# Two of three token tiles of the inner activation transposed by DMA instead of by TensorE

## The chip, the cores and the metric

The kernel runs on one core of one Trainium2 chip. Time is device time in microseconds (us). The kernel before took 1952.08 us, the median of three runs (1951.8 to 1953.06). The profile shown is of one further execution of the same program.

## The reference

One layer of a hybrid backbone is computed in float32 for 128 context tokens and 256 latent tokens, so 384 tokens with a model width of 2048: adaLN modulation, a mixing sub-layer (gated linear attention beside a Fourier branch), and a SwiGLU feed-forward sub-layer of hidden width 5632. Only the last of these bears on the change:

```python
h = rmsnorm(x, lw['norm_pre_ffn']) * (1.0 + sc2) + sh2
ff = (jax.nn.silu(h @ lw['w_ffn_gate']) * (h @ lw['w_ffn_up'])) @ lw['w_ffn_down']
x = x + ga2 * rmsnorm(ff, lw['norm_post_ffn'])
```

## The kernel before

Every float32 matrix product is made of three TensorE products: each operand is parted into a rounded high part and the rest (`whi`, `wlo` for weights), and high by high, high by low and low by high are added up. ScalarE rounds the high part (line 1430), VectorE subtracts to get the low part (line 1441), so each weight tile of 128x1024 costs one ScalarE pass and one VectorE pass before TensorE may use it.

The hidden width of the feed-forward part is worked through in eleven chunks of 512 columns, `c` = 0 to 10. From `c` = 1 on, the gate and up products of a chunk and the down products of the chunk before it are interleaved in one list, `steps` (lines 1338 to 1357). A step takes one weight tile. Its kind says what it computes. Kinds `A`, `B`, `C`, `E`, `F`, `G`, `H`, four steps each, are the gate and up products, arranged with sums and differences of token tiles and weights in the manner of Strassen's method, so that fewer products are needed. Kinds `D`, `DA` to `DH` are down products of chunk `c - 1`. The order in the part that matters is: H0, D6, H1, H2, D7, H3 of one chunk and then A0, A1, A2, A3, B0, B1, D4 of the next. A step of A has 12 matmuls (two token tiles), a step of H has 6, a step of D has 18.

The gate and up products come out with tokens on partitions and hidden columns along the free dimension. Once silu and the product are done, three tiles of 128 tokens x 512 float32 stand in the work tiles `g0`, `g1` and `s5` (token tiles 0, 1 and 2). The down product needs them the other way round, with hidden columns on partitions. `turn_hid` (lines 1591 to 1599) does that: four TensorE transposes of 128x128 float32 into one PSUM bank (line 1596, tile `ptr`), and then ScalarE and VectorE part the result into `hid_hi` and `hid_lo` (line 1598). In the main loop that is called behind the matmuls of A1, A2 and A3 for token tiles 1, 2 and 0 (line 1782). `hid_sums` (lines 1601 to 1610) forms sums and differences of the turned tiles 1 and 2 for the down product, and `hid_sums_lo` their low part.

The order on TensorE, ScalarE, VectorE and GpSimd is written out by hand; SyncE's is planned by the framework. Each step begins with `grab2` (line 1452): it takes the step's weight tile from a list of ready ones, issues what loads have room (`load_more`, on SyncE's queue), and calls `split_next` (line 1420), which makes the whi and wlo of a weight tile that is used three steps later. There are four buffers of each, so the ScalarE pass waits until TensorE has finished with the buffer of the step before. Work that is not weights is put off in a list, `pend`, and `split_next` takes three or four items from its head in each step (`settle_pend`), between the ScalarE pass and the VectorE pass. So an item that holds ScalarE or VectorE delays the weight passes behind it on that engine, in order.

Weights for A and B come through ten resident slots (loads `u`, line 1407), the others through two buffers `raw` (line 1399). `sum1` (line 1413) subtracts one resident slot from another on VectorE before the steps of B. The down sums of most chunks are added up in device memory by accumulating transfers that GpSimd issues (line 1642) out of tiles that ScalarE copies from PSUM (line 1638). VectorE also does the last adaLN map between all this (line 1474).

Of the kernel before, what the change touches and what calls it, by code (L numbers as in the profile page):

```python
# [11 lines left out]
F32 = mybir.dt.float32  # L12
F32R = mybir.dt.float32r
U32 = mybir.dt.uint32
AF = mybir.ActivationFunctionType
ALU = mybir.AluOpType
PSUM = bass.MemoryType.PSUM
# [3 lines left out]
P = 128  # L21
# [4 lines left out]
T = TC + TL  # L26
# [8 lines left out]
FC = 4  # L35
# [61 lines left out]
def tile_step(ctx: ExitStack, tc: tile.TileContext, a, o):  # L97
    nc = tc.nc
    PE, ACT, DVE, POOL, SP = nc.tensor, nc.scalar, nc.vector, nc.gpsimd, nc.sync
# [215 lines left out]
    psm = ctx.enter_context(tc.tile_pool(name="psm", bufs=3, space=PSUM))  # L315
    pss = ctx.enter_context(tc.tile_pool(name="pss", bufs=5, space=PSUM))
    with ExitStack() as s:
# [114 lines left out]
        for k in range(KT):  # L432
            sq = qs[k] if k < 2 else scr[:, 4 + k % 4, :]
# [178 lines left out]
    with ExitStack() as s:  # L612
# [9 lines left out]
        for c in range(2):  # L622
            src = a["a2"][:, 512 * c : 512 * c + 512]
# [192 lines left out]
        for c in range(2):  # L816

            dst = a2.rearrange("p (h d j) -> p d h j", d=2, j=P)[:, c]
# [29 lines left out]
    with ExitStack() as s:  # L848
# [166 lines left out]
        for b, i in mix_order:  # L1015
# [29 lines left out]
    with ExitStack() as s:  # L1045
# [49 lines left out]
        for i in range(KT):  # L1095
            p = psm.tile([P, T], F32, tag="mm", name="pmm")
# [193 lines left out]
        dt = {}  # L1290
# [11 lines left out]
        hid = hid_of()  # L1302
# [9 lines left out]
        pend, now = [], []  # L1312
# [26 lines left out]
        LAST = NFC - 1  # L1339
# [251 lines left out]
        def turn_hid(dst, t, pool, tag):  # L1591

            pt = pool.tile([P, FC, P], F32, tag=tag, name="ptr")
            src = (g0, g1, s5)[t]
            for j in range(FC):
                PE.transpose(pt[:, j, :], src[:, j * P : (j + 1) * P], ident)  # L1596
            hi, lo = (x[:, :, t * P : (t + 1) * P] for x in dst)
            pend.extend([lambda: ACT.copy(hi, pt), lambda: DVE.tensor_sub(lo, pt, hi.bitcast(F32))])  # L1598
# [88 lines left out]
        for kind, c, i in steps:  # L1687
            last_c = c == NFC - 1 and kind == "D"
            if last_c and hid_last is not None and x1b is None:
                while pend:  # L1690
                    pend.pop(0)()
                x1b = actp.tile([P, KT, T], F32, tag="A_hi", name="x1b")
                for q in range(4):
                    SP.dma_start(x1b[:, 4 * q : 4 * q + 4, :], x1_d[:, 4 * q : 4 * q + 4, :])
                ACT.activation(tmp1, eps_t, AF.Sqrt)
            if last_c and done >= 2:
                late_w.append(grab2())
                if len(late_w) == 4:
                    while pend:
                        pend.pop(0)()  # L1700
                continue
            if kind == "D":
                w = grab2()
                n, kh = i // 2, i % 2
                if kh == 0:
                    while pend:
                        pend.pop(0)()

                    pool, tag = (pss, "side") if done % 2 or (c, n) == (NFC - 2, 3) else (psm, "mm")
                    ts = (0, 1, 2) if last_c else (1, 2, 0)  # L1710
                    pd_tiles = {t: pool.tile([P, 512], F32, tag=tag, name="pdn") for t in ts}
                    d_live[0] += 3
                h = hid_last if last_c else hid
                todo = [
                    (pd_tiles[t], [[x[:, 2 * kh + m, t * P : (t + 1) * P] for m in range(2)] for x in h], mov_d, kh == 0, kh == 1)
                    for t in ts
                ]
                products(w, todo)
                if kh == 1:
                    if not last_c:  # L1720
                        for t in range(3):
                            if c < LAST - 1:
                                pend.append(lambda k=10 + 3 * (n - 2) + t, p=pd_tiles[t], c=c: to_sums(k, p, c))
                            else:
                                pend.append(lambda u=unit(t, n), p=pd_tiles[t]: out(u, p))
                    else:
                        for t in range(3):
                            pend.append(lambda t=t, n=n, p=pd_tiles[t], d=done: add_last(t, n, p, d))
                        if done == 1:
                            pend.append(lambda: DVE.tensor_add(r3, ssq[:, :, 0], ssq[:, :, 1]))  # L1730
                        done += 1
                if (c, i) == (NFC - 2, 6):

                    while pend:
                        pend.pop(0)()
                    hid_last = tuple(actp.tile([P, FC, T], F32R, tag=t, name="hidE") for t in ("C_hi", "C_lo"))
                    for t in range(3):
                        turn_hid(hid_last, t, psm, "mm")
                    for x in (0, 2, 4, 1, 3, 5):
                        pend[x]()  # L1740
                    pend.clear()
            elif kind[0] == "D":
                w = grab2()
                while pend:
                    pend.pop(0)()
                todo = []
                for n, stat, first, last in of_d[kind]():
                    if first:
                        d_bank[n] = psm.tile([P, 512], F32, tag="mm", name="pds")
                        d_live[0] += 1  # L1750
                    todo.append((d_bank[n], stat, mov_d, first, last))
                    if last:
                        pend.append(lambda k=PROD.index(n), p=d_bank[n], c=c: to_sums(k, p, c))
                products(w, todo, by_tile=kind in ("DB", "DC"))
            else:
                w = grab2()
                if kind == "H" and i == 0:
                    while pend:
# [12 lines left out]
                if (kind, c, i) == ("B", LAST, 0):  # L1771
                    while pend:
                        pend.pop(0)()
                    back = sums_back()
                if kind == "A" and i:
                    if c == 1 and i == 2:
                        while pend:
                            pend.pop(0)()
                        d_tiles()
                        load_more()  # L1780
                    if c > 1:
                        hid_pt.append(turn_hid(hid, i % 3, psm, "mm"))
                    if c < LAST and i == 2:
                        if c == 1:
                            f = dt["full"]
                            pend.append(lambda: DVE.tensor_add(f, hid[0][:, :, P:T].bitcast(F32), hid[1][:, :, P:T].bitcast(F32)))
                            pend.extend(hid_sums(f[:, :, 0:P], f[:, :, P:], DVE.tensor_copy))
                        else:
                            pend.extend(hid_sums(*hid_pt))
                    if i == 3:  # L1790
                        if c < LAST:
                            pend.insert(len(pend) - 1 if c > 1 else len(pend), hid_sums_lo)
                        hid_pt.clear()
                if (kind == "A" and i < 2) if turned[0] else c < LAST and kind + str(i) in ada_at:
# [177 lines left out]
```

## Time and profile before

| What | Value |
|---|---|
| median of 3 runs | 1952.08 us (1951.8 to 1953.06) |
| the profiled execution | 1951.26 us, span 1949.5 us |
| TensorE matmul busy | 1932.7 us, 99% of the span |
| VectorE busy | 1641.2 us, 84% |
| ScalarE busy | 1015.1 us, 52% |
| GpSimd busy | 145.2 us, 7% |
| TensorE transposes of `turn_hid` | 120, first at 1065.5 us, last at 1897.3 us |
| granted TensorE clock | 0.999 |

The profile is of one execution. PE is TensorE's matmuls, PEld its weight loads, DVE is VectorE, ACT is ScalarE, POOL is GpSimd, SPq the queue of SyncE. "whi<-u" names the tile written and the tile read. In lists of instructions in order of time, the first column is the start and the second the duration, both in us; an "x4" at the end of a row says that four like instructions were merged; a bracket gives idle time of the engine just before, and who ended it. The chain of work that ended last follows the end of the program back, at each step to what released it, and so says what the time was spent on.

### The profile page before, as it was taken

Reading aid. Unit: us, or ns where it says so; the run is one execution under the profiler, and the core shown is the slowest. Engines: PE = TensorE matmul, PEld = TensorE weight load, DVE = VectorE, ACT = ScalarE, POOL = GpSimd, SP = SyncE. Lnnn points to the kernel's source line nnn. Section 1 sums busy time; section 2 is a strip of 40 time slices with the busy share of each in tenths; the row PEclk is TensorE's granted clock in tenths of the full one; section 3 lists DMA queues with packets and bytes.
Section 4 is the critical chain, followed back from the end, with each engine's and each line's share of the span. In section 5 each row is a group of like instructions: output and inputs, shape, how many; then the busy total and the mean of one; then the engine's idle time right before and its main releaser. Section 6 shows DMA issues by size and latency. Waiting matters only on the chain.

```text
span 1949.5 us, 28077 instructions
## 1 busy us (share of the span) xinstructions
PE 1932.7 (99%) x10506; PEld 1712.5 (88%) x10506; DVE 1641.2 (84%) x2059; ACT 1015.1 (52%) x1477; POOL 145.2 (7%) x171
## 2 busy tenths in 40 slices
PE   8999999999999999999999999999999999999998
PEld 5779999999999999999988888888888888888886
DVE  5569888879876797978799999999999999988876
ACT  4233454554336655447455655555565565656445
POOL 0000000000000000004000111111111120211001
PEclk9999999999999999999999999999999999999999
DMA  9978677767754687655538686877868695959564
GB/s 390 370 262 265 228 251 230 229 224 257 252 189 159 213 277 247 211 175 182 169 128 261 148 252 153 236 185 204 213 193 225 175 236 168 248 128 241 151 205 130
DMA packets 217640, 422.05 MB, mean 216 GB/s; under 512 B 16796, under 2 KB 121436, under 8 KB 213152
## 3 DMA queue, kind: packets, MB, share of 16 engines
q1 hardware_dynamic: 199072, 386.70, 59.3%
q0 software_dynamic: 18432, 33.56, 11.4%
q8 instruction: 82, 1.34, 0.3%
q14 instruction: 54, 0.44, 0.1%
HBM read 365.68 MB, written 54.53 MB: 216 GB/s over the span
## 4 chain that ended last, share of the span: by engine, by line
PE 95%; DVE 2%; DMA 1%; ACT 1%; issue 0%; SPq 0%; POOL 0%; DVEq 0%; ACTq 0%; POOLq 0%
PE pmm L258 35%; PE pgu L1532 30%; PE pdn L1532 10%; PE pds L1532 7%; PE pv L398 3%; PE pgm L381 1%; PE pf L996 1%; DMA slab<-in_w_ada 1%; PE px L416 1%; PE pmm L1251 1%; PE ptr L1596 1%; PE pf L997 1%; PE bk L1532 1%; PE po L645 1%; DVE wlo L1441 0%
## 5 line engine op out<-in xcount | busy, mean ns | idle before, releaser
L258 PE MATMUL pmm<-A_hi,whi 128*128 128x384 f32 x1200 | 404.3, 337 | 0.0
L258 PE MATMUL pmm<-A_hi,wlo 128*128 128x384 f32 x1200 | 401.4, 334 | 0.0
L258 PE MATMUL pmm<-A_lo,whi 128*128 128x384 f32 x1200 | 401.3, 334 | 0.0
L1430 ACT CAST whi<-u 128x1024 fp32r<-128x1024 f32 x200 | 209.5, 1053 | 156.3 <-PE pgu L1532 53.7
L224 ACT CAST whi<-raw 128x1024 fp32r<-128x1024 f32 x181 | 189.7, 1051 | 176.1 <-DMA raw<-in_w_gate 53.3
L225 DVE TENSOR_TENSOR wlo<-raw,whi 128x1024 fp32r<-128x1024 f32 x179 | 217.9, 1220 | 52.3 <-ACT whi L224 51.9
L1430 ACT CAST whi<-raw 128x1024 fp32r<-128x1024 f32 x157 | 165.5, 1054 | 181.4 <-DMA raw<-in_w_d 48.5
L1441 DVE TENSOR_TENSOR wlo<-u,whi 128x1024 fp32r<-128x1024 f32 x200 | 242.2, 1218 | 17.4 <-ACT whi L1430 16.8
L1532 PE MATMUL pgu<-whi,A_hi 128*128 128x512 f32 x640 | 252.0, 394 | 0.0
L1532 PE MATMUL pgu<-whi,A_lo 128*128 128x512 f32 x640 | 249.5, 390 | 0.0
L258 PEld LDWEIGHTS pmm<-A_hi,whi 128*128 128x128 f32 x1200 | 225.3, 188 | 2.9 <-issue 1.4
L572 DVE SCALAR_TENSOR_TENSOR adacc<-adaw,spad,adacc 128x1024 f32<-128x1024 f32 x180 | 222.7, 1278 | 3.4 <-DMA adaw<-in_w_ada 3.2
L258 PEld LDWEIGHTS pmm<-A_lo,whi 128*128 128x128 f32 x1200 | 225.4, 188 | 0.2
L258 PEld LDWEIGHTS pmm<-A_hi,wlo 128*128 128x128 f32 x1200 | 225.2, 188 | 0.0
L1441 DVE TENSOR_TENSOR wlo<-raw,whi 128x1024 fp32r<-128x1024 f32 x157 | 191.3, 1219 | 17.6 <-ACT whi L1430 17.4
L1532 PE MATMUL pgu<-wlo,A_hi 128*128 128x512 f32 x640 | 185.9, 389 | 0.0
L1532 PEld LDWEIGHTS pgu<-whi,A_hi 128*128 128x128 f32 x640 | 120.1, 188 | 26.7 <-issue 1.2
L1532 PEld LDWEIGHTS pgu<-wlo,A_hi 128*128 128x128 f32 x640 | 120.2, 188 | 25.5
L1532 PEld LDWEIGHTS pgu<-whi,A_lo 128*128 128x128 f32 x640 | 120.2, 188 | 24.2
L1532 PE MATMUL pgu<-whi,S 128*128 128x512 f32 x400 | 117.6, 391 | 0.0
L1642 POOL DMA_DIRECT2D sums_d<-dw x64 | 58.6, 950 | 644.0 <-ACT dw L1638 638.7
L1532 PE MATMUL pdn<-whi,hid_hi 128*128 128x512 f32 x264 | 102.9, 390 | 0.2 <-DVE hid_lo L1598 0.2
(402 smaller groups left out, 3268.0 us busy)
## 6 DMA issues: line engine op xcount, KB each, us to landing
adaw<-in_w_ada SPq DMA_DIRECT2D x96, 512.0 KB, 4.2
raw<-in_w_d SPq DMA_DIRECT2D x70, 512.0 KB, 3.8
slab<-in_w_ada SPq DMA_DIRECT2D x32, 1024.0 KB
raw<-in_w_gate SPq DMA_DIRECT2D x64, 512.0 KB, 4.6
raw<-in_w_g SPq DMA_DIRECT2D x48, 512.0 KB, 4.2
raw<-in_w_u SPq DMA_DIRECT2D x48, 512.0 KB, 6.9
raw<-in_w_in SPq DMA_DIRECT2D x44, 512.0 KB, 5.0
u<-in_w_u SPq DMA_DIRECT2D x40, 512.0 KB, 7.5
```

Source lines behind the costliest of these rows:

```text
L224: ACT.copy(hi, raw)
L225: sub = lambda: eng.tensor_sub(lo, raw, hi.bitcast(F32))
L258: PE.matmul(dst, w[wi][:, k * n + n0 : k * n + n0 + P], x[xi][:, k0 + k, :], start=first and k == 0 and j == 0, stop=last and k == kts - 1 ...
L381: PE.matmul(pgv[q : q + 32, :], spad[:, k, :], slab[k // (KT // 2)][:, k % (KT // 2), :], start=k < 4, stop=k >= KT - 4,)
L398: PE.matmul(pv[2 * t + g], hT[x_][:, kb, t * P : (t + 1) * P], w_[:, g * 512 : (g + 1) * 512], start=kb == 0 and j == 0, stop=kb == KT - 1 ...
L416: PE.matmul(px, w_[:, u * P : (u + 1) * P], hT[x_][:, kb, :], start=j == 0, stop=j == 2)
L572: DVE.scalar_tensor_tensor(acc[:, c, :], w, spad[:, k, c : c + 1], acc[:, c, :], op0=ALU.mult, op1=ALU.add,)
L645: PE.matmul(dst, w[wi], x[xi], start=first and j == 0, stop=last and j == 2)
L1430: ACT.copy(hi, src)
L1441: DVE.tensor_sub(lo, src, hi.bitcast(F32))
L1532: PE.matmul(dst, stat[x_][m], mov(w[w_], m), start=first and w_ == m == x_ == 0, stop=last and w_ == m == 1, skip_group_check=any(more),)
L1642: POOL.dma_start(sums_d[k], u, accum_op=ALU.add)
```

## The change

The tiles of `g1` and `g0` (token tiles 1 and 0) of chunks 1 to 9 are no longer turned by TensorE. The transposing transfer moves 16-bit elements, so a float32 tile of 128x512 is handled as 128x1024 halves:

- `apart`: ScalarE copies the tile so that all lower halves stand in front and all upper halves behind (into `e2` or `sq`, which are free there), and then issues on its own queue a transposing transfer of 128x1024 16-bit elements, from that tile back to `g1` or `g0`.
- `together`: ScalarE copies the two turned planes of halves so that they are float32 numbers again (into `e2`, and for tile 0 into `g1`).
- `hid_parts`: ScalarE and VectorE part the joined tile into `hid_hi` and `hid_lo`, as before, but from SBUF and not from PSUM.

`apart` of g1 is put in `pend` behind the matmuls of H0, that of g0 behind H1; `together` of g1 behind A0, that of g0 behind A2. Token tile 2 (`s5`) is still turned by TensorE, now behind A1. `hid_sums` reads tile 1 from `e2`. The last chunk is turned by TensorE in all three tiles, as before.

```diff
+        Q_DMA = ACT
+
+        def apart(src, mid, dst):
+
+            def op():
+                ACT.copy(
+                    mid.bitcast(U16).rearrange("p (h c) -> p h c", h=2), src.bitcast(U16).rearrange("p (c h) -> p h c", h=2),
+                )
+                Q_DMA.dma_start(dst.bitcast(U16).rearrange("p (a t) -> p a t", t=P), mid.bitcast(U16), transpose=True)
+
+            return op
+
+        def together(src, dst):
+
+            return lambda: ACT.copy(
+                dst.bitcast(U16).rearrange("p (x h) -> p h x", h=2), src.bitcast(U16).rearrange("p (h x) -> p h x", h=2),
+            )
+
+        def hid_parts(t, src):
+
+            hi, lo = (x[:, :, t * P : (t + 1) * P] for x in hid)
+            src = src.rearrange("p (j c) -> p j c", j=FC)
+            return [lambda: ACT.copy(hi, src), lambda: DVE.tensor_sub(lo, src, hi.bitcast(F32))]
...
-                    if c > 1:
-                        hid_pt.append(turn_hid(hid, i % 3, psm, "mm"))
-                    if c < LAST and i == 2:
-                        if c == 1:
...
-                        else:
-                            pend.extend(hid_sums(*hid_pt))
-                    if i == 3:
+                    if c == 1 and i == 2:
...
+                if c < LAST:
+                    if (kind, i) == ("H", 0):
+                        pend.append(apart(g1, e2, g1))
+                    elif (kind, i) == ("H", 1):
+                        pend.append(apart(g0, sq, g0))
+                if c > 1 and kind == "A":
+                    if i == 0:
+                        pend.append(together(g1, e2))
+                    elif i == 1:
+                        hid_pt.append(turn_hid(hid, 2, psm, "mm"))
+                        pend.extend(hid_parts(1, e2))
+                    elif i == 2:
+                        pend.append(together(g0, g1))
                         if c < LAST:
-                            pend.insert(len(pend) - 1 if c > 1 else len(pend), hid_sums_lo)
+                            pend.extend(hid_sums(e2.rearrange("p (j c) -> p j c", j=FC), hid_pt.pop()))
+                    else:
                         hid_pt.clear()
+                        pend.extend(hid_parts(0, g1))
+                        if c < LAST:
+                            pend.append(hid_sums_lo)
```

More of the change, by code (lines that the diff above doesn't have):

```diff
@@ L14 @@
 U32 = mybir.dt.uint32
+U16 = mybir.dt.uint16
 AF = mybir.ActivationFunctionType
@@ L1780, in tile_step @@
                         load_more()
-                    if c > 1:
-                        hid_pt.append(turn_hid(hid, i % 3, psm, "mm"))
-                    if c < LAST and i == 2:
-                        if c == 1:
-                            f = dt["full"]
-                            pend.append(lambda: DVE.tensor_add(f, hid[0][:, :, P:T].bitcast(F32), hid[1][:, :, P:T].bitcast(F32)))
-                            pend.extend(hid_sums(f[:, :, 0:P], f[:, :, P:], DVE.tensor_copy))
-                        else:
-                            pend.extend(hid_sums(*hid_pt))
-                    if i == 3:
+                    if c == 1 and i == 2:
+                        f = dt["full"]
+                        pend.append(lambda: DVE.tensor_add(f, hid[0][:, :, P:T].bitcast(F32), hid[1][:, :, P:T].bitcast(F32)))
+                        pend.extend(hid_sums(f[:, :, 0:P], f[:, :, P:], DVE.tensor_copy))
+                    if i == 3 and c == 1:
+                        pend.append(hid_sums_lo)
[12 more added lines that the diff above has]
+                        pend.append(together(g0, g1))
                         if c < LAST:
-                            pend.insert(len(pend) - 1 if c > 1 else len(pend), hid_sums_lo)
+                            pend.extend(hid_sums(e2.rearrange("p (j c) -> p j c", j=FC), hid_pt.pop()))
+                    else:
                         hid_pt.clear()
+                        pend.extend(hid_parts(0, g1))
+                        if c < LAST:
+                            pend.append(hid_sums_lo)
                 if (kind == "A" and i < 2) if turned[0] else c < LAST and kind + str(i) in ada_at:
```

## The prediction

> **What bounds the kernel now.** I read the page's busy times and its chain first, then the chain of one chunk change, then busy times by stage, and last what ScalarE, SyncE and VectorE do in the stage that the change touches.
>
> ```profile
> PE 1932.7 (99%) x10506; PEld 1712.5 (88%) x10506; DVE 1641.2 (84%) x2059; ACT 1015.1 (52%) x1477; POOL 145.2 (7%) x171
> PE 95%; DVE 2%; DMA 1%; ACT 1%; issue 0%; SPq 0%; POOL 0%; DVEq 0%; ACTq 0%; POOLq 0%
> ```
>
> TensorE is the bound over the whole span: the chain is 95% TensorE's own work, so time taken off TensorE comes off the end, as long as nothing else falls behind. The change takes such work off. What it costs there is in the chain of waits around one chunk change (start, length, what; A1 ends the first piece, A2 and A3 are the pieces of twelve, B0 and B1 the 24, D4 the 18):
>
> ```profile
> 1249.97 3.18 PE pgu L1532 x14
> 1253.15 0.44 PE ptr L1596 x4
> 1253.58 2.77 PE pgu L1532 x12
> 1256.35 0.44 PE ptr L1596 x4
> 1256.79 2.77 PE pgu L1532 x12
> 1259.56 0.44 PE ptr L1596 x4
> 1260.00 5.49 PE pgu L1532 x24
> 1265.48 4.08 PE pdn L1532 x18
> ```
>
> A turn of four transposes holds the chain for 0.44 us, and the twelve matmuls behind it take 2.77 us where undisturbed ones take 4.08/18 = 0.2267 us each, 2.72 us for twelve. So a turn costs 0.44 + 0.05 = 0.49 us.
>
> The stage from H0 to D4 of this change of chunk, split at A0/A1 and D4, and the rest of the chunk (columns: stretch, its length, then busy us of PE, PEld, DVE, ACT, POOL, then clock, busy share of the DMA engines, GB/s):
>
> ```profile
> 1233.00:1250.00 17.00, 17.00 (x76) 13.91 (x75) 16.97 (x22) 11.04 (x14) 4.49 (x6) 1.00 1.05 308
> 1250.00:1266.00 16.00, 16.00 (x77) 13.19 (x76) 14.38 (x17) 10.07 (x13) 0.00 (x0) 1.00 0.48 116
> 1266.00:1326.00 60.00, 60.00 (x266) 49.72 (x265) 56.87 (x56) 34.21 (x42) 10.52 (x12) 1.00 0.81 207
> sum 93.00, PE 93.00 PEld 76.82 DVE 88.22 ACT 55.32 POOL 15.01; mean PE 31.00 PEld 25.61 DVE 29.41 ACT 18.44 POOL 5.00
> ```
>
> VectorE has 93.00 - 88.22 = 4.8 us to spare in a chunk, ScalarE 37.7 us. In the first stretch, where the transfers will be issued, VectorE is full and so are the DMA engines (1.05, 308 GB/s).
>
> **The change part by part.** *TensorE.* Two turns of three go in nine chunks, 18 turns or 72 of the 120 transposes: 18 x 0.49 = 8.8 us less. The 0.44 alone would give 7.9 us.
>
> ```profile
> L1596 PE MATMUL ptr<-ident,ep x120: 270/272/273, 1065.7 to 1897.4; 128*128 128x128 f32 x120
> L1598 ACT CAST hid_hi<-ptr x27: 572/583/590, 1068.2 to 1819.9; 128x512 fp32r<-128x512 f32 x27
> L1585 DVE TENSOR_TENSOR ep<-ep,ep x10: 692/693/696, 1049.4 to 1879.5; 128x512 f32<-128x512 f32 x10
> L1598 DVE TENSOR_TENSOR hid_lo<-ptr,hid_hi x27: 681/691/693, 1068.8 to 1820.5; 128x512 fp32r<-128x512 f32 x27
> ```
>
> One transpose lasts 272 ns, but they run into one another, so durations are not what is saved. The Trainium skill, "TensorE: Matmul & The Clock Gate", Part 4, gives about 275 ns for a 128x128 transpose in a kernel's context; the duration here agrees (272 ns), but the chain shows 0.49/4 = 0.12 us of it on the path. Taken as the price, the page's figure would make 72 x 275 ns = 19.8 us, an estimate.
>
> ScalarE's weight passes around the change of chunk, and below them TensorE's first matmul of A1 and its first with A1's wlo, then VectorE's passes that make wlo:
>
> ```profile
> 1236.61 1.06 ACT L1430 CAST whi<-raw 128x1024 fp32r<-128x1024 f32 x1
> 1238.22 1.05 ACT L1430 CAST whi<-u 128x1024 fp32r<-128x1024 f32 x1 [0.56 <-PE pdn L1532]
> 1240.49 1.05 ACT L1430 CAST whi<-u 128x1024 fp32r<-128x1024 f32 x1 [1.21 <-PE pgu L1532]
> 1241.85 1.06 ACT L1430 CAST whi<-u 128x1024 fp32r<-128x1024 f32 x1 [0.30 <-PE pgu L1532]
> 1245.02 1.06 ACT L1430 CAST whi<-u 128x1024 fp32r<-128x1024 f32 x1 [2.12 <-PE pdn L1532]
> 1251.10 1.05 ACT L1430 CAST whi<-u 128x1024 fp32r<-128x1024 f32 x1 [2.21 <-DVE u L1413]
> 1255.51 1.05 ACT L1430 CAST whi<-raw 128x1024 fp32r<-128x1024 f32 x1 [0.61 <-ACT hid_hi L1598]
> 1250.26 0.39 PE L1532 MATMUL pgu<-whi,A_hi 128*128 128x512 f32 x1
> 1252.08 1.07 PE L1532 MATMUL pgu<-wlo,A_hi 128*128 128x512 f32 x4
> L1441 DVE TENSOR_TENSOR wlo<-u,whi 128x1024 fp32r<-128x1024 f32 x200 | 242.2, 1218 | 17.4 <-ACT whi L1430 16.8
> ```
>
> *Parting and joining, ScalarE and VectorE.* `hid_parts` does what line 1598 did, from SBUF: VectorE's subtraction takes 693 ns between SBUF tiles and 691 ns from PSUM, so nothing. New are two passes of 1024 halves for each of the 18 tiles. ScalarE's rows above have 1024 elements a partition in 1.05 us; strided 16-bit ones are not in the trace, so bounds are half and twice that, and I take 1.05 us, the row with as many elements: 36 x 1.05 = 37.8 us, 4.2 us a chunk of the 37.7 us to spare. What decides is not the sum but the place. The first five rows make the weights of D7, H3, A0, A1 and A2; the sixth of B0, the seventh of D4. `apart` of g1 falls behind the first row (it is taken up in D6's `grab2`), that of g0 behind the third. Both passes fit into the time in brackets, in which ScalarE waited; whi is made three steps ahead.
>
> *Issuing on ScalarE's queue.* The kernel issues no DMA there yet, and the issue holds ScalarE for X us while the weight passes queue behind it. Nearest rows:
>
> ```profile
> L1407 SPq DMA_DIRECT2D u<-in_w_g x40: 367/368/832, 915.1 to 1801.0; - x40
> L1642 POOL DMA_DIRECT2D sums_d<-spare x64: 865/1216/1577, 1098.7 to 1807.2; - x64
> sums_d<-spare POOLq DMA_DIRECT2D x64, 256.0 KB, 6.7
> ```
>
> X lies between 0.37 us (a plain 512 KB load on SyncE's hardware queue) and 6.7 us (all the time that a 256 KB transfer takes to land, if the queue is held until then); GpSimd's issue takes 1.2 us. With g1 parted by 1238.6, H3's whi starts at 1238.6 + X, A0's follows 0.95 later, g0 is parted by 1241.5 + X, and A1's whi is done by 1242.5 + 2X. TensorE uses it at 1250.26, so X up to 3.9 us costs nothing; A1's wlo, 1.22 us later, is wanted at 1252.08 and gives 4.1. (Passes of twice 1.05 us would lower 3.9 to 2.8.) Above 3.9 each chunk stalls 2X - 7.8 us. I take 1.2 us: it is an issue of the same size, and anything under 3.9 gives the same sum. Cost 0; at X = 6.7, 9 x 5.6 = 50 us.
>
> The Trainium skill has two answers on how fast a transposing transfer is. "Advanced Engine Details and Errata", X-Bar Transpose (TRN2), calls it as fast as a regular one, 350 to 400 GB/s: 256 KB in 0.7 us, an estimate, and the sum stands. "VectorE: DVE Perf Modes", The three transpose paths, has 1309 ns for one 128x128 block of 16-bit elements: eight in a row are 10.5 us, an estimate, and if ScalarE were held for that, 9 x (21.0 - 7.8) = 119 us slower before the gain. No row before shows either.
>
> *The wait in front of joining.* `together` of g1 comes after B0's whi (ends 1252.15), that of g0 after D4's (1256.56). Issued by 1238.6 + X and 1241.5 + 2X, the transfers have over 12 us each; the 6.7 us row fits, so nothing. Later than that, ScalarE waits with B's weights behind it.
>
> Three loads that fall into the same time, their landing, and the subtractions that use them:
>
> ```profile
> 1239.22 2.10 SPq L1407 DMA_DIRECT2D u<-in_w_g  x2
> 1244.55 0.37 SPq L1407 DMA_DIRECT2D u<-in_w_g  x1
> u<-in_w_g SPq DMA_DIRECT2D x4, 512.0 KB, 8.7
> 1252.05 1.21 DVE L1413 TENSOR_TENSOR u<-u,u 128x1024 f32<-128x1024 f32 x1
> 1261.12 1.22 DVE L1413 TENSOR_TENSOR u<-u,u 128x1024 f32<-128x1024 f32 x1
> ```
>
> *DMA engines.* A chunk gets two transfers of 256 KB, 0.5 MB, 1.7 us at 308 GB/s, into a full stretch. Behind them may stand the loads of B1 to B3, issued at 1239.22 to 1244.55, which VectorE's subtractions at 1252.05 to 1261.12 want. B1 lands at 1239.2 + 8.7 = 1247.9, 4.1 us early; B3 at 1253.3, 7.8 us early. A delay of 1.7 us costs nothing. If the small pieces of a transpose keep the engines longer, a delay beyond 4.1 us makes VectorE wait, and beyond 4.1 + 4.8 = 8.9 us a chunk TensorE.
>
> *VectorE as the next bound.* A chunk shrinks by 0.97 us, VectorE's spare time from 4.8 to 3.8. `hid_lo` of tile 1 no longer waits for a turn, and that of tile 0 moves ahead of `hid_sums_lo`. Cost 0.
>
> *SyncE.* Its order is planned anew, but no load is added or taken; cost 0, its loads having the slack just shown.
>
> **Sum.** -8.8 us, bounds -7.9 and +41 (-8.8 + 50). The profiled execution would go from 1951.26 to 1942.5; it lies 0.8 us under the median of 1952.08, which goes to 1943.3.
>
> **Rivals.**
>
> 1. *ScalarE held by its transfers; slower.* The place is H0 to A1. It decides at X = 3.9 us, and at 4.4 us the gain is gone. At 6.7 us: 1952.1 + 41 = 1993. For it: this queue has never issued here, and the engines are full just then. Against: issues on SyncE and GpSimd are done in 0.37 and 1.2 us while their transfers take 6.7 to 8.7.
> 2. *Transposes crowd the loads; slower.* It decides at 8.9 us of delay a chunk. With each transfer filling the engines for its 6.7 us: 9 x (13.4 - 8.9) = 40 us, so 1983. For it: share 1.05, and 16-bit elements. Against: the next stretch is only 0.48 busy.
> 3. *VectorE sets the pace; no change.* It has 16.97 of 17.00 us of work in the first stretch, so a slip of ScalarE can't be made up there. If each chunk loses the 0.97 us again, 1952. Against: TensorE is at 17.00 of 17.00 beside it, so VectorE runs full while it is ahead.
> 4. *The whole duration is saved.* 72 x 272 ns = 19.6 us, 1932.5. The chain speaks against it. The Trainium skill's 275 ns, from "TensorE: Matmul & The Clock Gate", would have it so.
>
> **How the numbers follow.** The forecast has 0.72 (its own range 1941 to 1948), rival 1 has 0.07, rival 2 has 0.10, rival 3 with partial losses 0.09, rival 4 has 0.02. A measurement of this kernel can tell about 0.2%, 4 us, from no change. Faster: 0.72 + 0.02 = 0.74; same: 0.09; slower: 0.17. To leave out no more than 2 in 10 the range runs from 1940 over rival 3 into the mild ends of 1 and 2 (X to 4.9 us, +10 us): 1962.
>
> **What would show it.** Right: 48 `ptr` transposes, a chain piece of 48 matmuls from A2 to B1, DMA rows on ScalarE's queue well under 3.9 us, joining copies that wait for no DMA, TensorE still at 99%. Wrong: weight loads of TensorE that wait for whi at A1 (rival 1), line 1413 waiting for `u` loads (rival 2), waits for wlo (rival 3). The prediction fails most easily on X, which no row of before holds.

## The result, and the profile after

The changed kernel took 1948.62 us, the median of 16 runs (1946.78 to 1953.04), the kernel before 1952.85 us beside it (16 runs, 1949.9 to 1957.8). The ratio is 0.9979 with a 95% interval of [0.9972, 0.9987]: 4.2 us, 0.21%, less. The forecast was 8.8 us less. The direction is right, but half of the gain did not arrive. The profiled execution took 1949.2 us (span 1947.4) against 1951.26 (span 1949.5).

From the page of the changed kernel, its busy times, its queue of transposing transfers (packets, MB, share of 16 engines) and its chain:

```profile
PE 1926.3 (99%) x10434; PEld 1704.9 (88%) x10434; DVE 1639.7 (84%) x2059; ACT 1049.6 (54%) x1513; POOL 145.2 (7%) x171
...
q10 hardware_dynamic: 19008, 4.72, 1.6%
...
PE 84%; DMA 5%; issue 4%; DVE 4%; ACT 2%; POOL 0%; SPq 0%; ACTq 0%; DVEq 0%; POOLq 0%
```

TensorE has 72 instructions less (10506 to 10434) and is still at 99%, but the chain has fallen from 95% TensorE to 84%, with 5% on transfers of all kinds, loads of weights among them: followed back from the end, it now leaves TensorE at several late loads and at one late transposing transfer. The transposing transfers themselves are small, 4.72 MB and 1.6% of the engines' span, which makes about 1.7 us of all 16 engines for each of the 18.

The new work, from the list of what touches the `ep` tiles (duration min/median/max in ns, first and last start in us):

```profile
L1597 PE MATMUL ptr<-ident,ep x48: 270/272/328, 1066.6 to 1895.5; 128*128 128x128 f32 x48
L1607 ACT COPY ep<-ep x18: 1035/1044/1049, 1051.9 to 1800.2; 128x1024 uint16<-128x1024 uint16 x18
L1610 ACTq DMA_TRANSPOSE ep<-ep x18: 1248/1309/1785, 1052.9 to 1801.3; - x18
L1616 ACT COPY ep<-ep x18: 1327/1360/1369, 1068.6 to 1815.5; 128x1024 uint16<-128x1024 uint16 x18
DMA to landing us min/median/max: 9.0/10.6/12.1
```

Parting takes 1.04 us and issuing holds ScalarE for 1.31 us, close to the 1.05 and 1.2 of the prediction; joining takes 1.36. A transfer needs 9.0 to 12.1 us to land where the trace has the landing (four of the eighteen), not the 6.7 of GpSimd's row. By the packets of all eighteen, the last data arrives 8.1 to 14.7 us after the issue, median 9.1.

What waited, from 1040 us on (engine, line, for whom: us in total, times, longest):

```profile
ACT ep L1607 <- DVE ep L1587: 18.2, 9, 2.2
DVE acc L1475 <- DMA w<-in_w_ada: 7.4, 4, 4.4
ACT ep L1616 <- DMA ep<-ep: 4.3, 3, 2.9
PEld pgu L1533 <- ACT ep L1574: 4.0, 2, 2.6
PEld pgu L1533 <- ACT whi L1431: 2.8, 5, 1.5
```

The first row is a wait that the prediction did not have: parting g1 stands behind the product of line 1587 that makes g1, and ScalarE waits up to 2.2 us for it in front of each of the nine partings. It delays the first issue (1241.00 in the chunk below, not 1238.6) and nothing on TensorE. The others matter.

To see where time goes, I took from each trace the start of the first matmul of D7 and of D4, chunk by chunk: the piece between them holds the turns. (At the ninth change D0 stands in D4's place.) Undisturbed, this piece is exactly 0.97 us shorter than before. Seven of the nine changes of chunk are. The first is 1.59 us longer and the third 1.54 longer, so 2.56 and 2.51 us were lost there; everything else between 985 and about 1890 us adds 1.6.

**The third change of chunk**, ScalarE and its queue in order of time:

```profile
1239.92 1.05 ACT L1607 COPY ep<-ep 128x1024 uint16<-128x1024 uint16 x1 [2.17 <-DVE ep L1587]
1241.00 1.25 ACTq L1610 DMA_TRANSPOSE ep<-ep  x1
...
1244.19 1.04 ACT L1607 COPY ep<-ep 128x1024 uint16<-128x1024 uint16 x1
1245.27 1.76 ACTq L1610 DMA_TRANSPOSE ep<-ep  x1
...
1260.60 1.33 ACT L1616 COPY ep<-ep 128x1024 uint16<-128x1024 uint16 x1 [2.90 <-DMA ep<-ep]
...
1262.06 1.08 ACT L1574 COPY ep<-pgu 128x512 f32<-128x512 f32 x2
```

and TensorE at its end:

```profile
1262.70 0.50 PE L1533 MATMUL pgu<-whi,A_hi 128*128 128x512 f32 x1 [2.21 <-ACT ep L1574]
```

The second transfer was issued at 1245.27 and landed 15.3 us later. Joining tile 0 waited 2.90 us for it. Behind it on ScalarE stand the two copies that empty A's PSUM banks (line 1574), and TensorE needs such a bank almost at once: of the 2.9 us, 2.2 arrive there. The slack at this place is about 0.7 us (2.90 - 2.21).

**The first change of chunk**, VectorE in order of time:

```profile
1062.14 1.42 DVE L1475 SCALAR_TENSOR_TENSOR acc<-w,spad,acc 128x512 f32<-128x512 f32 x2 [4.38 <-DMA w<-in_w_ada]
1063.47 2.36 DVE L1442 TENSOR_TENSOR wlo<-u,whi 128x1024 fp32r<-128x1024 f32 x2
1065.74 0.68 DVE L1590 TENSOR_TENSOR ep<-ep,pgu 128x512 f32<-128x512 f32 x1
1066.34 1.22 DVE L1414 TENSOR_TENSOR u<-u,u 128x1024 f32<-128x1024 f32 x1
```

and ScalarE and TensorE beside it, each from its own list:

```profile
1067.65 1.05 ACT L1431 CAST whi<-u 128x1024 fp32r<-128x1024 f32 x1 [4.33 <-DVE u L1414]
```

```profile
1066.57 0.63 PE L1597 MATMUL ptr<-ident,ep 128*128 128x128 f32 x4 [0.63 <-DVE ep L1590]
```

Here no join is late. A 256 KB load of adaLN weights, issued at 1053.39 just behind the first transfer, kept VectorE waiting for 4.38 us. Two low-part passes, the last product of tile 2 and line 1414 stand behind it in VectorE's order. Line 1414 held up ScalarE's weights for 4.33 us, and the product held up the turn of tile 2. On TensorE three waits follow: 0.23 us for a low part at 1064.75, the 0.63 above, and 0.93 at 1074.96 for the evictions of line 1574, which ScalarE, late and with both joins to do, reaches at 1074.33.

The same load in the trace of before, in VectorE's list:

```profile
1059.48 1.42 DVE L1474 SCALAR_TENSOR_TENSOR acc<-w,spad,acc 128x512 f32<-128x512 f32 x2 [1.14 <-DMA w<-in_w_ada]
```

There it cost TensorE nothing; 1.14 us of VectorE's spare time were already used up by it. The median landing of these loads, before and with the change (six and nine of the 64 have a landing in the trace):

```profile
w<-in_w_ada SPq DMA_DIRECT2D x64, 256.0 KB, 5.4
```

```profile
w<-in_w_ada SPq DMA_DIRECT2D x64, 256.0 KB, 7.2
```

### The profile page after: what moved, and what is told of

It reads as the page before. It is cut to its first block, busy times and chain, and to the rows that moved or that the text cites. A ratio compares the mean times of both kernels' runs of the same rounds, so it can differ in the third digit from the quotient of the medians.

```text
span 1947.4 us, 27999 instructions
## 1 busy us (share of the span) xinstructions
PE 1926.3 (99%) x10434; PEld 1704.9 (88%) x10434; DVE 1639.7 (84%) x2059; ACT 1049.6 (54%) x1513; POOL 145.2 (7%) x171
## 3 DMA queue, kind: packets, MB, share of 16 engines
q10 hardware_dynamic: 19008, 4.72, 1.6%
## 4 chain that ended last, share of the span: by engine, by line
PE 84%; DMA 5%; issue 4%; DVE 4%; ACT 2%; POOL 0%; SPq 0%; ACTq 0%; DVEq 0%; POOLq 0%
PE pmm L259 35%; PE pgu L1533 23%; PE pdn L1533 8%; PE pds L1533 5%; PE pv L399 3%; PE pgm L382 1%; DMA raw<-in_w_u 1%; DVE wlo L1442 1%; DMA slab<-in_w_ada 1%; PE pf L997 1%; PE px L417 1%; PE pmm L1252 1%; DMA ep<-ep 1%; ACT whi L1431 1%; PE bk L1533 1%
```

## The experiments

Where the other half went, the two places above suggest two theories, and ScalarE's new work is a third. A: a transfer lands late, and the join that waits for it delays the evictions behind it. B: the transfers crowd other transfers, the adaLN loads most, and these come late, whoever reads the turned tiles. C: ScalarE's 36 new passes delay the weights behind them. If it is A alone or C alone, traffic that nobody waits for costs nothing; if it is C, the loss stays when the transfers go. Each run is compared with the kernel before run beside it on the same chip; differences are of medians. Beside that I give for the profiled execution the sum of the nine D7-to-D4 pieces against its control, and that of everything else between 985 and about 1890 us:

| Run | Control | Nine changes of chunk, us | The rest, us |
|---|---|---|---|
| the changed kernel | before | -3.7 | +1.6 |
| e1_no_turn | before | -8.6 | -1.2 |
| e2_no_transfer | before | -8.8 | +1.2 |
| e3_unused | before | +4.6 | +1.8 |
| e4_one_tile | before | -3.8 | +1.5 |
| e6_skip_first | before | -5.6 | +2.7 |
| e7_free_evict | before | -6.6 | +6.1 |
| e8_late_both | before | -7.8 | +4.2 |
| e10_after_noada | e9 | -8.1 | +0.6 |
| e12_after_early | e11 | -8.8 | +1.1 |
| e13_after_ask | e14 | -8.0 | +2.4 |

In e6 and e8 only eight of the nine changes are turned by transfer. e1 and e2, which have no transfer, show how far the rest moves by itself, -1.2 to +1.2 us.

### e1: no turns, no passes, no transfers

```diff
-                if c < LAST:
-                    if (kind, i) == ("H", 0):
-                        pend.append(apart(g1, e2, g1))
-                    elif (kind, i) == ("H", 1):
-                        pend.append(apart(g0, sq, g0))
...
-                        pend.append(together(g1, e2))
...
-                        pend.extend(hid_parts(1, e2))
+                        pend.extend(hid_parts(1, g1))
...
-                        pend.append(together(g0, g1))
...
-                        pend.extend(hid_parts(0, g1))
+                        pend.extend(hid_parts(0, g0))
```

> The 18 turns on TensorE are gone as in the change, but nothing takes their place: no copies of halves, no transfers, and the parts are taken straight from g1 and g0, so tiles 1 and 0 stay unturned in the down product. All theories that accept the chain (0.49 us a turn) expect 8.8 us less than before, 1944, and every change of chunk 0.97 us shorter. If a turn is worth less than the chain says, it is the 4 us that the change gave, 1948.5.

Measured: 1941.67 us against 1951.98, 0.9946 [0.9934, 0.9958], so 10.3 us less. All nine changes of chunk are shorter, eight by 0.97 and the last by 0.84. The gain of 0.49 us a turn is there in full once nothing has to be paid for it, with 1 to 2 us above the forecast that lie outside the turns.

### e2: the passes stay, the transfers go

```diff
-                Q_DMA.dma_start(dst.bitcast(U16).rearrange("p (a t) -> p a t", t=P), mid.bitcast(U16), transpose=True)
...
-                        pend.append(together(g1, e2))
+                        pend.append(together(e2, g1))
...
-                        pend.append(together(g0, g1))
+                        pend.append(together(sq, e2))
```

(Two readers of the joined tiles are renamed to match.)

> Turns gone, the four copies of halves in each chunk kept (the second undoes the first), the transposing transfers left out, so tiles 1 and 0 stay unturned. Theory A (the second transfer lands after its join is due, and ScalarE stands before the evictions of A that TensorE waits for) and theory B (the transfers crowd the weight loads) both expect the whole 8 to 9 us, 1944. Theory C (ScalarE's copies alone, 1.04 and 1.36 us, push the evictions back) expects no more than about 4 us less than before, 1948.5, with TensorE waiting for the evictions at B0.

Measured: 1943.03 us against 1951.98, 0.9953 [0.994, 0.9966], 9.0 less. Nine clean changes. The 36 passes cost about 1.4 us (1943.03 - 1941.67, and the two intervals overlap): C is not it. What is between this and the changed kernel, 0.9953 against 0.9979, about 5 us, came with the transfers.

### e3 and e5: transfers that nobody reads, added to the kernel before

```diff
+                if c < LAST and kind == "H" and i < 2:
+                    dst, n = ((s1, 8), (xd, 6))[i]
+                    pend.append(lambda dst=dst, n=n: ACT.dma_start(
+                        dst.bitcast(U16).rearrange("p (a t) -> p a t", t=P), spad16[:, 0 : n * P], transpose=True,
+                    ))
```

> The kernel before with all its turns, and beside them two transposing transfers a chunk that nobody reads (from a constant tile; one of full size, one of three quarters), issued on ScalarE's queue where the change issues its own. No copies of halves, no joins. Theory B expects 2 to 4 us more than before (1955 to 1957), with waits for weight loads in the steps behind B1. Theory A expects no more than 0.5 us, 1953, since nobody waits for the landing.

Measured: 1958.44 us against 1951.98, 1.0035 [1.0023, 1.0046], 6.5 more, where B had expected 2 to 4. No join exists here and nobody waits for these transfers, and still they cost more than the changed kernel loses. A alone is refuted. The adaLN wait in the trace of e3 and the instruction that has it, from the waits and from VectorE's list:

```profile
DVE acc L1475 <- DMA w<-in_w_ada: 6.1, 1, 6.1
```

```profile
1064.81 1.42 DVE L1475 SCALAR_TENSOR_TENSOR acc<-w,spad,acc 128x512 f32<-128x512 f32 x2 [6.13 <-DMA w<-in_w_ada]
```

That load was issued at 1054.38 and VectorE could go on 10.4 us later. 4.6 us of the loss stand in this one change of chunk, 1.8 are spread. Not all of the 4.6 is waiting: TensorE waits 2.19 us there for a low part, and behind that its granted clock (the column ahead of the DMA share) is near one half:

```profile
1067.50:1071.00 3.50, 3.50 (x11) 2.86 (x12) 3.50 (x4) 0.66 (x1) 0.00 (x0) 0.52 0.84 305
```

The stretch at 0.50 lasts 3.41 us, so about 1.7 us of the 4.6, an estimate, are slow matmuls. The trace of the changed kernel has none there: behind its longest wait of TensorE (2.21 us, at 1262.70) the clock stays at 1.00. So in this execution the waits alone took less than e3's time says.

e5 is the same edit with one block (32 KB) in each transfer in place of eight and six: `((s1[:, 0:64], 1), (xd[:, 0:64], 1))[i]`.

> As the kernel with unused transfers, but each moves one block of 128x128 halves (32 KB) and not six or eight. If it is the traffic that costs (the small pieces of the transfers keep the adaLN and weight loads back), the 6.7 us of the unused transfers go to within 1 us of the time before, 1953. If it is what the issue does to ScalarE's queue, most of it stays, 1957 or more.

Measured: 1953.83 us against 1952.02, 1.0008 [0.9999, 1.0017]. The number of transfers and their places in ScalarE's order are those of e3; the cost falls from 6.5 to 1.8 us, with an interval from 0 to 3.3. So most of it comes with the traffic and not with the number of issues on ScalarE's queue. The issues themselves got shorter too, 1.11 us against 1.77 in the median, and what ScalarE's longer hold adds in e3 the pair doesn't separate.

### e4: only tile 1 by transfer

```diff
-                    elif (kind, i) == ("H", 1):
-                        pend.append(apart(g0, sq, g0))
...
-                        pend.append(together(g0, g1))
...
-                        pend.extend(hid_parts(0, g1))
+                        turn_hid(hid, 0, psm, "mm")
```

> Token tile 1 goes by transfer, tile 0 is turned by TensorE as before. Theory A (it is the second transfer that is late) expects no wait for a landing and the whole of nine turns, 4.4 us less than before, 1948.4, as fast as the change with two tiles. Theory B expects half of the crowding, so about 3.4 us less. If the first transfer is late too, 2 us less, 1950.8.

Measured: 1950.94 us against 1951.98, 0.9993 [0.9984, 1.0001], 1.0 less. Under every theory I had expected more. The trace has no late join; eight changes are 0.49 shorter, the first 0.15 longer with a 3.4 us wait of VectorE for an adaLN load. By the medians, half of the transfers keep less than half of the gain; the interval, from 3.1 us less to 0.2 more, includes half.

### e6: the first change of chunk left to TensorE

```diff
-                if c < LAST:
+                if 1 < c < LAST:
                     if (kind, i) == ("H", 0):
...
-                if c > 1 and kind == "A":
+                if c == 2 and kind == "A" and i:
+                    hid_pt.append(turn_hid(hid, i % 3, psm, "mm"))
...
+                if c > 2 and kind == "A":
```

> The change, but for the tiles of chunk 1, which TensorE turns as before: 16 turns gone and not 18. If the loss of the first change of chunk comes from the adaLN load that has no slack there (it landed 5.4 us after its issue before, 8.7 with the transfers) it goes, 2.6 us, and 0.97 us of gain is given up: 1.6 us less than the change, 1947. If the loss is spread over the chunks evenly (about 5 us over nine), 0.4 us more than the change, 1949.

Measured: 1949.5 us against 1952.02, 0.9985 [0.9976, 0.9993]. If the first change of chunk were the place of the loss, leaving it out should have won. It did not: in this trace a late join costs 2.1 us at the seventh change (at 1632 us), and three of the stretches between lose about 1 us each to weights. Which chunk pays varies from kernel to kernel; that some do, does not.

### e7 and e8: evictions that stand behind no join

`sq` and `g1` change roles from chunk to chunk, so that the eviction copies write no tile that a transfer still uses, and the join of tile 0 moves behind them:

```diff
+        def roles(c):
+
+            return (ep[1], ep[4]) if c % 2 else (ep[4], ep[1])
...
-                        pend.append(together(g1, e2))
+                        pend.append(together(roles(c - 1)[1], e2))
...
-                        pend.append(together(g0, g1))
...
-                        pend.extend(hid_parts(0, g1))
+                        pend.append(together(g0, roles(c - 1)[0]))
+                        pend.extend(hid_parts(0, roles(c - 1)[0]))
```

> The change with the work tiles' roles rotated, so that the evictions of A write to tiles that no transfer is using, and the join of tile 0 put behind these evictions. If the late landing of the second transfer costs through the evictions that stand behind the join (2.5 us at the third change of chunk in the profile), TensorE no longer waits for line 1574 there, and the time is 1 to 3 us less than with the change, 1946 to 1947.5. If late joins are rare or cost through other things, no difference, 1948.6.

Measured: 1951.85 us against 1952.02, 0.9996 [0.9987, 1.0005]: the gain is gone. TensorE waits for no eviction any more, but in the first change of chunk the turned tile 0 is now late for D4, which multiplies it. From the waits of e7, from 1065 us on:

```profile
PEld pdn L1533 <- ACT hid_hi L1630: 2.1, 2, 1.9
PE pdn L1533 <- ACT hid_hi L1630: 1.5, 1, 1.5
```

There the wait moved from the banks of A to the first use of the tile. Earlier in the same change of chunk, at 1062.76, VectorE had waited 5.0 us for an adaLN load, and behind the 1.5 us on TensorE the clock is at one half again, for 3.41 us:

```profile
1084.00:1087.00 3.00, 3.00 (x9) 2.35 (x8) 3.00 (x3) 0.74 (x1) 0.00 (x0) 0.50 0.00 0
```

That is about 1.7 us (an estimate) of the 6.1 in "the rest". The other eight changes of chunk are clean. So in this one trace a late load, the late tile and a slow stretch fall together; how much of the lost gain of the median is due to the place of the join stays open. e8 has this edit and that of e6 together.

> Both edits: chunk 1 turned by TensorE, roles rotated and the join of tile 0 behind the evictions. If both causes are right, the eight other changes of chunk give 7.8 us less than before and only the background of waits for weight loads stays: 1944.5 to 1946. If neither is, 1949.

Measured: 1948.33 us against 1952.02, 0.9983 [0.9974, 0.9992], 3.7 less. Its eight turned changes are all clean (-7.8 = 8 x 0.97), with no late join and no late eviction, and still the rest adds 4.2 us, partly waits at D4 of 0.06 to 0.45 us a chunk, partly weights (1.2 us of it stand at 1044 us, ahead of the first transfer). So the joins are one way in which the gain is lost, and not the only one.

### e9 and e10: the adaLN loads left out of both kernels

```diff
-                    SP.dma_start(w, a["w_ada"][m - 2, q // 2, k, :, 512 * (q % 2) : 512 * (q % 2) + 512])
+                    if q == 0 and k < 2:
+                        SP.dma_start(w, a["w_ada"][m - 2, q // 2, k, :, 512 * (q % 2) : 512 * (q % 2) + 512])
```

> The kernel before, with 62 of the 64 loads of the last adaLN weights left out (VectorE multiplies what the first two left, at the same points; the last modulation is therefore not the reference's). It is the control of the next run. Its own time tells what these loads cost without any transfer: in the trace of before VectorE waits for one of them at the first change of chunk (1.14 us) and TensorE does not, so 0 to 1 us less than before, about 1952.

> The changed kernel with the same 62 loads left out. If the loss comes mainly over these loads (a transfer delays a load, VectorE waits for it in its order, and what VectorE does next is late for TensorE), the distance to the control is -7 to -9 us, near the -8.8 forecast. If it comes mainly over the joins that stand in front of the evictions and over the inner weights, the distance stays at -4 to -5. Half and half: about -6.5.

Measured: 1951.15 us for the control (11 runs, 1949.79 to 1952.71) and 1941.18 us for the change on top of it (5 runs, 1940.19 to 1943.07); against before, whose median was 1952.16, ratios of 0.9994 [0.9985, 1.0003] and 0.9945 [0.9933, 0.9958]. The change gives 10.0 us here, where it gave 4.2 with the loads in place. Without transfers these loads cost 1.0 us (the interval includes nothing), with the transfers 7.4 (1948.6 - 1941.2, the 1948.6 from another chip). Landing of the transfers in e10, in the same view as above, and the chain around the third change of chunk:

```profile
DMA to landing us min/median/max: 7.3/7.5/10.5
```

```profile
1244.65 6.80 PE pgu L1534 x30
1251.45 0.43 PE ptr L1598 x4
1251.89 10.93 PE pgu L1534 x48
1262.82 4.08 PE pdn L1534 x18
```

This is the chain that the prediction drew: one turn, then 48 matmuls from A2 to B1 without a gap, then D4. Eight of nine changes are 0.97 shorter, the last 0.29. By the packets of all eighteen, the last data comes 5.4 to 10.6 us after the issue, median 7.8, instead of 8.1 to 14.7, median 9.1; no join waits for its transfer. The same ten microseconds in the windows of the changed kernel and then of e10, which runs 2 us ahead here (stretch, length, busy us of PE, PEld, DVE, ACT, POOL, then clock, DMA share, GB/s):

```profile
1256.00:1266.00 10.00, 7.79 (x34) 6.12 (x33) 7.33 (x10) 6.18 (x9) 0.00 (x0) 1.00 0.60 92
```

```profile
1256.00:1266.00 10.00, 10.00 (x46) 8.28 (x45) 9.41 (x13) 6.42 (x9) 0.00 (x0) 1.00 0.15 53
```

In the changed kernel the engines are still at 0.60 here with TensorE idle for 2.2 us; in e10 they are at 0.15 and the transfers are done.

### e11 and e12: two adaLN steps moved out of the way

```diff
-        ada_at = ('B2', 'E0', 'E2', 'F0', 'G1', 'G3', 'H0', 'H2')
+        ada_at = ('B2', 'E0', 'E2', 'F0', 'F2', 'G0', 'G1', 'G3')
```

> The kernel before, with the two adaLN steps of H0 and H2 of each chunk done at F2 and G0. The control of the next run. VectorE is nearly full there too, so 0 to +2 us against before.

> The changed kernel with the same two steps moved, so that the adaLN loads of a chunk are asked for ahead of the transfers. If these loads are where most of the loss comes from, and asking earlier is enough, the distance to the control is -6 to -8. If they are not, or if the DMA engines are so full that the order of asking does not matter, it is -4 to -5, as between the two kernels themselves.

Measured: the control 1956.1 us, 1.0018 [1.0009, 1.0027], the change on top 1948.35 us, 0.9979 [0.997, 0.9988]. The distance is 7.8 us, as theory B had it, and all nine changes are clean (-8.8). But the control lost 3.9 us by the move, more than the 0 to 2 expected, presumably since VectorE's products are now in a place that is worse for the weights, so nothing is won over the changed kernel.

### e13 and e14: the loads asked for earlier, VectorE's order kept

With the moved steps two things had changed at once. So here only the issue moves, by one step:

```diff
+                    for n in (range(2) if k == 0 else range(k + 1, min(k + 2, KT))):
+                        SP.dma_start(wt[:, n % 2, :], a["w_ada"][m - 2, q // 2, n, :, 512 * (q % 2) : 512 * (q % 2) + 512])
-                    SP.dma_start(w, a["w_ada"][m - 2, q // 2, k, :, 512 * (q % 2) : 512 * (q % 2) + 512])
```

> The changed kernel with every adaLN load but the first two of a quarter issued one step earlier, ahead of VectorE's products of the step before, while these products stay where they are. The transfers' traffic and the loads' traffic are what they were; only the slack of these loads grows, by one step. If the loss of the change is that these loads come late for VectorE, 1943 to 1945 (the control less 8 or 9). If the loss is the traffic itself, which delays the joins and the inner weights whenever 256 KB more are under way, no less than 1947.

> The control: the kernel before with the same earlier issue. VectorE's waits for these loads are small in its trace (1.14 us at the first change of chunk, none of it on TensorE), so 1952, as before.

Measured: 1947.35 us (9 runs, 1942.24 to 1951.06), 0.9972 [0.9962, 0.9983], and the control 1952.71, 1.0001 [0.9992, 1.001]: a distance of 5.4 us. From the waits of e13, from 1065 us on:

```profile
PEld pgu L1534 <- ACT whi L1431: 4.1, 5, 2.1
...
ACT ep L1617 <- DMA ep<-ep: 2.2, 2, 1.2
...
DVE acc L1476 <- DMA w<-in_w_ada: 0.6, 1, 0.6
```

From 1040 us on, with the first change of chunk, VectorE's wait for the loads is down from 7.4 to 0.6 us, and the changes of chunk are clean but for the last (-8.0). Yet by the medians only 1.2 us of the 5.8 that e10 recovers come back. The larger part therefore seems to be not that these loads are late, but that they are there: with them under way the transfers and the weights come later (joins still wait 2.2 us, and TensorE waits 4.1 us for high parts of weights, 4.6 from 1040 us on, where the changed kernel has 2.8). It is the best median of the kernels that do all the work, but its interval overlaps that of the changed kernel, which ran beside other copies of before; I don't call it faster.

## Why the prediction was half right

- **TensorE, 18 x 0.49 us: right.** Every undisturbed change of chunk is 0.97 us shorter, in ten traces (the changed kernel and nine of the experiments; 0.49 in e4, which turns one tile less). Neither 0.44 nor the 0.272 of a transpose's duration is the price. The Trainium skill's 275 ns ("TensorE: Matmul & The Clock Gate", Part 4) stands there beside a transpose of 16-bit elements; it is again the duration that the trace shows for float32 (272 ns), and not what goes when a transpose goes. Rival 4, 1932.5, is out.
- **Parting and joining, 0: right in effect.** e2 against e1 puts them at about 1.4 us, for 36 passes of 1.04 and 1.36 us. That parting g1 waits for line 1587 was missed, and cost nothing by itself.
- **Issuing on ScalarE's queue, X = 1.2, cost 0: right as far as e5 can tell.** X is 1.25 to 1.79 us, far below 3.9. Rival 1 did not come, and e5 puts the issues, with little traffic, at 1.8 us, with an interval from 0 to 3.3.
- **DMA engines, 0: this is the step that failed.** I divided bytes by throughput, 0.5 MB at 308 GB/s, 1.7 us a chunk, and found 4.1 us of slack at the `u` loads of B1 to B3. By the trace each transfer is 1024 data packets of 256 bytes, but their own time is not the loss either: 1.6% of the engines' span is about 3.5 us a chunk, still under the slack that I had counted. What I left out is that the adaLN loads under way beside them take longer, and so I counted the slack at the wrong loads. In e3 two such transfers a chunk, which no one reads, cost 6.5 us. The term measures about 5 us (the changed kernel against e2) where I had 0.
- **Rival 2 named the mechanism and the wrong place and size.** It looked at the `u` loads, which had slack, and set the threshold at 8.9 us a chunk. What broke first were the adaLN loads: in the trace of before VectorE already waited 1.14 us for one of them, a row that the prediction did not use. That one had no slack to count, and the median landing went from 5.4 to 7.2 us. With the adaLN loads out, the crowding costs nothing that shows (e10: -10.0).
- **The wait in front of joining, 0: failed with it.** I gave a landing 6.7 us from a transfer of equal size on another queue and allowed over 12. It is 9.0 to 12.1, once 15.3 by the join that waited; the second transfer's packets begin only when the first's have ended, and both share full engines. Three of the 18 joins waited, 4.3 us in all. I also had weights behind the join; what stands there first are the evictions of line 1574, with about 0.7 us of slack. e7 and e8, which move the join, are not faster than the changed kernel; in e7's trace the wait is then at D4.
- **VectorE as the next bound: not by its load.** It is at 84% as before. It passes on a late load because it works in order, which is how the first change lost 2.56 us.

The Trainium skill's two figures for such a transfer measure different things on the same rows. "Advanced Engine Details and Errata", X-Bar Transpose (TRN2), has it as fast as a regular one, 0.7 us for 256 KB as an estimate. By its packets the fastest transfer here moved its data in 1.0 us (e10, 1063.83 to 1064.79), which is near; but its first packet came 4.4 us after the issue, and beside the loads the data took 3.5 to 9.1 us in the changed kernel. "VectorE: DVE Perf Modes", The three transpose paths, has 1309 ns a block, 10.5 us for eight as an estimate. The median landing of the changed kernel (10.6 us) agrees, but by luck: it is 7.5 us in e10, and one block alone landed in 5.4 to 6.8 us in e5. ScalarE is held for 1.31 us in the median and not for the whole transfer.

What stays open: how the 5 us divide between late joins, VectorE's order and weights. It differs from trace to trace, and the rest outside the changes moves by about 1.2 us either way even without transfers. That the transfers stretch because their small packets take turns with the 1 to 2 KB packets of the loads fits all runs, but packet size alone was not varied.

## What to carry to other kernels

A transfer's cost beside full DMA engines is not its bytes over the throughput, and here not the time of its own packets either: look for the load with the least slack in the same stretch, not for the one that the edit makes you think of. Here it was the load for which an engine already waited a little before the change. Work that moves from the bounding engine to the DMA engines should first be tried with the traffic alone (e3) and with the competing load taken away (e10): the two runs together say what the gain is and what takes it. Read the granted clock stretch by stretch beside the waits, since a slow stretch behind a wait adds to it (e3).

## What the runs showed of the hardware that I had not expected

- A transposing transfer of 128x1024 16-bit elements between SBUF tiles sends its first data packet 3.0 to 4.1 us after the issue in the changed kernel when no other is under way (1241.00 to 1245.07 in the third change of chunk) and, behind another, only when that one has ended (1250.95 and 1250.96); its data take 1.0 us at best (e10) and 9.1 at worst (the changed kernel); its last data comes 5.4 us after issue at best (e10) and 14.7 at worst (the changed kernel).
- Its issue holds ScalarE's queue for 1.25 to 1.79 us in the changed kernel, also where the data comes 14.7 us later; in e3 for up to 2.95 us.
- A strided pass of 16-bit elements costs ScalarE 1.04 us for 1024 elements when the reads are strided, 1.36 us when the writes are; the contiguous float32 pass takes 1.05.
- The same 62 adaLN loads cost 1.0 us without the transfers and 7.4 us with them.
- The granted clock of TensorE fell to 0.50 for 3.41 us behind a wait of 2.19 us (e3) and of 1.51 us (e7), and stayed at 1.00 behind one of 2.21 us (the changed kernel). What decides it no run here shows.
